# Letting an engine's computed order wait for a far more urgent instruction

## The chip, the cores and the metric

The kernel runs on one core of one Trainium2 chip. The metric is the device time of one execution in microseconds (us); lower is better. The core's engines are PE (TensorE, matrix products), DVE (VectorE), ACT (ScalarE), POOL (GpSimd) and SP (SyncE, which here only issues transfers). Each takes its instructions in the sequence in which the program gives them.

## What is computed

Two trunk layers over 512 latent tokens and 256 context tokens of width 1024. In each layer one projection feeds three attention groups of eight heads and a gate; their results are gated, projected back and added to the stream. Cut to what matters:

```python
def layer(x, cx, ...):
    hx = rmsnorm(x, norm_w) * (1 + scale) + shift        # scale, shift, gate from c @ ada_w + ada_b
    hc = rmsnorm(cx, norm_w) * (1 + scale_c) + shift_c
    px, pc = split_cols(hx @ w_in), split_cols(hc @ w_in)
    ya, yca = global_gqa(...)           # A: all latent and context keys
    yb, ycb = neighbourhood_attn(...)   # B: 2-D window, relative bias
    yc, ycc = window_gqa(...)           # C: +-128 tokens, a sink logit per head
    x = x + gate * ((concat(ya, yb, yc) * silu(px[9])) @ w_out)
    ...                                 # the same for cx, in layer 0 only
    return x, cx
```

After the second layer a final RMSNorm gives the output.

## The kernel before

**The work.** Activations lie transposed (features on partitions, tokens along the free dimension). Every float32 operand of a product is split into a high part, rounded to the matrix format, and a low part, the remainder; a product is three matmuls (high x high, high x low, low x high). So a weight tile of 128x512 is loaded by SP (ws, L254 or L500), rounded by ACT (wh, L245), and its remainder is computed by DVE or POOL (wl, L248). In the output projection of layer 0 some of these tiles are called kept.

An attention unit computes scores on PE into the bank Sbig; DVE scales or masks them and takes the row maximum (P and negm, L1115 to L1117 for group A, L1218 for C, L1278 for B); ACT takes the exponential (L1118, L1221, L1280); SP copies P into a tile of the matrix format (R<-P, L1044); PE transposes R (T, L1049); ACT and DVE make the high and low part (pth L781, ptl L1029); PE multiplies with the values (Obig, L1033). The queries of A and C get their rotary factors on POOL (L951 to L953) with a copy of rotated rows that SP makes (tB<-tA, L950, four issues a tile). At the end of a layer, gated head outputs (u) are loaded again and split (hL, qt, kt and ut, L480 and L481) for the output projection (L508). The modulation vectors of layer 1 are computed on the side, in part as dot products on DVE (junk, L154), over 512 columns in the attention stage and 1024 in the output projection.

The stages in time: a start (to about 97 us) with normalisation and the first projections, the attention of layer 0 woven with the projections of the next heads, its output projection (from about 540 to 660 us), the same for layer 1, and the last output projection and norm.

**What sets the order.** Program text gives only the dependencies. `arrange` (L1950) collects all instructions as `Step` objects with modelled lengths (`busy`, the time for which the engine is taken; `move`, a transfer's length; `ISSUE`, the length of a DMA's issue by its target, 430 ns otherwise). `Graph.run` (L1771) is a simulated execution that places them one by one. For each engine there are two heaps: `later` holds steps whose predecessors are all placed, with the time at which they are ready; `now` holds those that are ready by the engine's current time `t`. The step in `now` with the smallest rank is taken. A step that opens a tile may have to wait for a buffer of its pool (`held`, woken when a buffer comes free). `Graph.back` (L1900) goes through the run backwards and gives each step the time from the end at which it must have started; the negative of it is the next turn's rank, in ns, so a smaller rank means more urgent. The first turn ranks by program priority. This is repeated `turns` = 6 times, and the sequences of the turn that is shortest on paper are fixed as dependencies between neighbours on each engine. PE's sequence comes out of the same run, with a rule of its own that keeps transposes together.

The modelled lengths and delays (`WAIT`, `BEHIND`, `TO_PE`, `TO_LAND`, L1596 to L1600) are constants: the flight of a transfer is a fixed part, its length, and what the other rings take meanwhile.

Of the kernel before, what the change touches and what calls it, by code (L numbers as in the profile page):

```python
# [1594 lines left out]
BANKS = ("pj", "T", "Sbig", "Obig")  # L1595
TO_PE, TO_OTHER, TO_LAND = 400.0, 150.0, 700.0  # L1596
SLOW = 21000.0
ISSUE = dict(tB=580.0, R5=520.0, R2=520.0, wr=680.0)
WAIT = {"PE": 53.0, "POOL": 78.0, "ACT": 36.0, "DVE": 36.0, "SP": 30.0}
BEHIND = {"ACT": 112.0, "DVE": 85.0, "POOL": 45.0}  # L1600
# [13 lines left out]
class Step:  # L1614
# [16 lines left out]
    def cost(self, tiles):  # L1631
# [7 lines left out]
        if self.dma:  # L1639
            b = 4 * outs[0][2][0][1] * size(outs[0][2])  # L1640
            out = stem(outs[0][0].name).split("_")[0]
            far = any(u[0].name not in tiles or tiles[u[0].name][1] for u in ins)
            self.busy = ISSUE.get(out, 430.0)
            self.fixed = 2400.0 if far else 1650.0
# [49 lines left out]
class Graph:  # L1694
# [76 lines left out]
    def run(self, rank):  # L1771

        steps, n = self.steps, len(self.steps)
# [3 lines left out]
        later = {e: [] for e in ENGINES.values()}  # L1777
        now = {e: [] for e in ENGINES.values()}
        free = {e: 0.0 for e in ENGINES.values()}
# [23 lines left out]
        while done < n:  # L1803
            t, e = min((max(free[e], -1.0 if now[e] else later[e][0][0]), e) for e in later if now[e] or later[e])
            free[e] = t = max(t, free[e])
            while later[e] and later[e][0][0] <= t:
                _, r, k = heapq.heappop(later[e])
# [9 lines left out]
                    heapq.heappush(now[e], ((-1e18, 0), min(same)[1]))  # L1817
            r, k = heapq.heappop(now[e])
            s = steps[k]
            need, wait = t, None  # L1820
            for name in self.opens[k]:
                tag = self.tag[name]
# [32 lines left out]
            elif e == "PE":  # L1855
# [5 lines left out]
                if row > 2 and s.switch > 5:  # L1861
                    busy += 20
                if t < SLOW:
                    busy *= 2
# [27 lines left out]
            for j in self.after[k]:  # L1892
                x = fin + self.gap(s, steps[j]) if self.before[j][k] else t
# [175 lines left out]
```

## Time and profile before

| | |
|---|---|
| time, median of 3 runs | 1146.3 us (1142.51 to 1149.14) |
| the profiled execution: time | 1148.5 us |
| the profiled execution: span from first to last instruction | 1146.7 us |
| mean granted clock of TensorE | 0.992 |
| instructions | 21341 |
| bytes moved by DMA | 200.96 MB, mean 175 GB/s |

The profile is one execution. A row of the timeline or of the chain begins with its start and its length in us; then come the engine, the line, the operation, and the tiles written and read (out<-in), and in brackets how long the engine stood idle before it and for whom. A row of the waits names who waited for whom, then the total in us, the number of times and the longest. A row of the windows gives the stretch, its length, and then the busy time of PE, of PE's weight loads (PEld), DVE, ACT and POOL with their instructions, the granted clock, the busy share of the DMA engines and GB/s. Issues of DMAs stand under SPq. Some rows hold several instructions (x3), and their length reaches from the first to the last.

### The profile page before, as it was taken

How to read it: one execution, taken by the hardware profiler on the slowest of the kernel's cores; microseconds unless marked ns; L12 is line 12 of the kernel's file. 1: busy time of each engine (PE TensorE's matmuls, PEld its weight loads, DVE VectorE, ACT ScalarE, POOL GpSimd, SP SyncE). 2: the span in 40 equal slices, each digit the busy share in tenths (PEclk: the TensorE clock that was granted, in tenths of full speed). 3: DMA queues.
4: the chain of work that ended last, by engine and by line, in shares of the span. 5: the costliest groups of instructions: out<-in, count | busy, mean ns of one | idle time of the engine just before them, and what ended most of it. 6: DMA issues, size and time to landing. Idle time of an engine off the chain costs nothing.

```text
span 1146.7 us, 21341 instructions
## 1 busy us (share of the span) xinstructions
PE 1106.9 (97%) x7352; PEld 974.5 (85%) x7352; DVE 778.3 (68%) x1642; ACT 675.8 (59%) x1454; POOL 401.1 (35%) x352
## 2 busy tenths in 40 slices
PE   5999999999999999999899999999999999999996
PEld 3799989998888888888687989998988888888886
DVE  5767667656657777668879764778565567677753
ACT  5546556465656667768623643555556677778651
POOL 1542102145452364526400021221156656556001
PEclk8999999999999999999999999999999999999998
DMA  9455446445464555456768543555344554557452
GB/s 356 180 154 191 140 135 193 137 152 165 157 204 151 191 174 185 160 186 217 252 227 267 166 148 98 169 182 152 126 144 157 161 180 163 194 177 228 140 175 74
DMA packets 111541, 200.96 MB, mean 175 GB/s; under 512 B 13676, under 2 KB 32456, under 8 KB 111432
## 3 DMA queue, kind: packets, MB, share of 16 engines
q1 hardware_dynamic: 103440, 184.01, 49.3%
q10 hardware_dynamic: 7992, 15.58, 4.1%
q8 instruction: 58, 0.95, 0.4%
q14 instruction: 51, 0.42, 0.1%
HBM read 116.46 MB, written 11.25 MB: 111 GB/s over the span
## 4 chain that ended last, share of the span: by engine, by line
PE 79%; DMA 6%; DVE 5%; ACT 3%; issue 3%; POOL 3%; SPq 1%; ACTq 0%; DVEq 0%; POOLq 0%
PE pj L311 29%; PE Obig L1033 9%; PE Sbig L1033 9%; PE T L1049 6%; PE pj L332 6%; PE pj L508 5%; DMA R<-P 4%; PE T L508 4%; PE Sbig L508 2%; PE Sbig L419 2%; PE T L311 2%; PE pj L419 1%; DVE junk L154 1%; PE Sbig L332 1%; DMA dw<-adat_dram 1%
## 5 line engine op out<-in xcount | busy, mean ns | idle before, releaser
L311 PE MATMUL pj<-hL,wh 128*128 128x512 f32 x880 | 293.1, 399 | 0.7 <-ACT tR L995 0.5
L1029 DVE TENSOR_TENSOR ptl<-T,pth 128x512 fp32r<-128x512 f32 (+1 forms) x264 | 172.5, 670 | 70.4 <-ACT pth L781 68.2
L781 ACT ACTIVATE pth<-T 128x512 fp32r<-128x512 f32 (+1 forms) x264 | 147.3, 580 | 73.3 <-PE T L1049 64.4
L311 PEld LDWEIGHTS pj<-hL,wh 128*128 128x128 f32 x880 | 158.8, 188 | 27.3 <-issue 1.7
L311 PE MATMUL pj<-hL,wl 128*128 128x512 f32 x440 | 174.8, 397 | 0.0
L245 ACT ACTIVATE wh<-ws 128x512 fp32r<-128x512 f32 x192 | 119.9, 629 | 93.1 <-PE pj L311 37.4
L1033 PE MATMUL Sbig<-kt,qt 128*128 128x256 f32 (+1 forms) x864 | 159.4, 305 | 0.9 <-DVE negm L1218 0.8
L248 POOL TENSOR_TENSOR wl<-ws,wh 128x512 fp32r<-128x512 f32 x76 | 100.2, 1320 | 145.1 <-ACT wh L245 126.0
L1033 PEld LDWEIGHTS Sbig<-kt,qt 128*128 128x128 f32 x864 | 127.6, 189 | 11.2 <-DVE negm L1218 1.8
L1049 PEld LDWEIGHTS T<-identr,R 128*128 128x128 f32 x1024 | 106.8, 140 | 27.4 <-DMA R<-P 7.4
L1033 PE MATMUL Obig<-pth,vt 128*128 128x256 f32 (+2 forms) x432 | 125.9, 307 | 2.2 <-DVE OT L1069 1.5
L1033 PE MATMUL Obig<-ptl,vt 128*128 128x256 f32 (+2 forms) x432 | 123.8, 306 | 0.2
L1049 PE MATMUL T<-identr,R 128*128 128x128 f32 x1024 | 114.5, 242 | 8.4 <-DMA R<-P 7.2
L248 DVE TENSOR_TENSOR wl<-ws,wh 128x512 fp32r<-128x512 f32 x116 | 84.9, 738 | 40.2 <-ACT wh L245 30.0
L311 PE MATMUL pj<-hC,wh 128*128 128x256 f32 x512 | 98.8, 284 | 0.0
L311 PEld LDWEIGHTS pj<-hL,wl 128*128 128x128 f32 x440 | 82.7, 188 | 15.0 <-issue 0.9
L1033 PEld LDWEIGHTS Obig<-pth,vt 128*128 128x128 f32 x432 | 81.3, 188 | 10.1 <-DVE OT L1069 2.1
L1033 PEld LDWEIGHTS Obig<-ptl,vt 128*128 128x128 f32 x432 | 81.2, 188 | 6.1 <-DVE negm L1117 0.5
L311 PEld LDWEIGHTS pj<-hC,wh 128*128 128x128 f32 x512 | 82.1, 190 | 2.1 <-DVE rs L881 0.2
L1115 DVE CUSTOM_DVE_ANT_0 P<-Sbig,rs 128x768 f32<-128x768 f32 (+1 forms) x80 | 65.7, 845 | 25.5 <-PE Sbig L1033 17.9
L1118 ACT ACTIVATE P<-P,negm 128x768 f32<-128x768 f32 (+1 forms) x80 | 67.5, 846 | 22.5 <-DVE negm L1117 16.7
L1459 POOL TENSOR_TENSOR bm<-wr,bm 128x192 f32<-128x192 f32 (+1 forms) x48 | 41.6, 893 | 97.3 <-DMA bm<-mskB_dram 64.6
(340 smaller groups left out, 2288.4 us busy)
## 6 DMA issues: line engine op xcount, KB each, us to landing
R<-P SPq DMA_DIRECT2D x216, 256.0 KB
ws<-wf_dram SPq DMA_DIRECT2D x120, 256.0 KB
ada<-adaw_dram SPq DMA_DIRECT2D x32, 512.0 KB
ws<-wo_dram SPq DMA_DIRECT2D x57, 256.0 KB
bm<-mskB_dram SPq DMA_DIRECT2D x16, 576.0 KB
R<-P SPq DMA_DIRECT2D x64, 128.0 KB
ws<-wt_dram SPq DMA_DIRECT2D x24, 256.0 KB
tB<-tA SPq DMA_DIRECT2D x72, 64.0 KB
```

The source lines that it names most:

```text
L245: nc.scalar.activation(hi, src, AF.Copy)
L248: eng.tensor_sub(lo, src, hi.bitcast(F32))
L311: nc.tensor.matmul(p[:, 0:n], a[:, r, :], cols(b[kt], c0, n), start=(i == 0), stop=(i == 23))
L332: nc.tensor.matmul(p[:, t * 256:(t + 1) * 256], tok(a[kt], t2 + t), b[:, r, :], start=(i == 0), stop=(i == 23))
L508: nc.tensor.matmul(p[:, 0:n], a[:, r, :], ucols(ua[b][ft], c0, n), start=(ft == FT_ORDER[0] and i == 0), stop=(ft == FT_ORDER[-1] and i == 2))
L781: nc.scalar.activation(out, src, AF.Copy)
L1029: nc.vector.tensor_sub(lo[:, 0:n], T[:, 0:n], hi[:, 0:n].bitcast(F32))
L1033: return nc.tensor.matmul(*args, **kw)
L1049: return nc.tensor.transpose(out.bitcast(F32R), src, identr)
L1115: nc.vector.tensor_tensor_reduce(out=P, in0=S, in1=r.to_broadcast([128, n]), op0=OP.mult, op1=OP.max, scale=1.0, scalar=-3.0e38, accum_out=m)
L1118: nc.scalar.activation(P, P, AF.Exp, bias=nm, accum_out=unit.stat("sums", i))
L1459: nc.gpsimd.tensor_add(b, src, b)
```

## The change

A table `HOLD` gives for DVE, ACT, POOL and SP, but not PE, a gap in rank of 3000 ns. When the run has taken the step with the smallest rank `r` for such an engine, it looks through `later` for steps whose rank is smaller by more than the gap and that become ready before the taken step would end (for a DMA: before the longer of its issue and its transfer would end). If there are any, `x` is the earliest of their times. Among the ready steps (the taken one included), those whose `busy` ends by `x + 60` ns may still go, the most urgent of them first; if there is none, the engine's time is set to `x` and nothing is placed. Everything else is as before: the instructions, the tiles, the number of turns, the choice among them.

```diff
@@ -1595,6 +1595,7 @@
 BANKS = ("pj", "T", "Sbig", "Obig")
 TO_PE, TO_OTHER, TO_LAND = 400.0, 150.0, 700.0
 SLOW = 21000.0
+HOLD = dict(DVE=3000.0, ACT=3000.0, POOL=3000.0, SP=3000.0)
 ISSUE = dict(tB=580.0, R5=520.0, R2=520.0, wr=680.0)
@@ -1817,6 +1818,20 @@
                     heapq.heappush(now[e], ((-1e18, 0), min(same)[1]))
             r, k = heapq.heappop(now[e])
             s = steps[k]
+            if e in HOLD:
+                long = max(s.busy, s.move) if s.dma else s.busy
+                soon = [x for x, y, _ in later[e] if y[0] < r[0] - HOLD[e] and x < t + long]
+                if soon:
+                    x = min(soon)
+                    fit = [z for z in now[e] if t + steps[z[1]].busy <= x + 60]
+                    heapq.heappush(now[e], (r, k))
+                    if not fit:
+                        free[e] = x
+                        continue
+                    r, k = min(fit)
+                    now[e].remove((r, k))
+                    heapq.heapify(now[e])
+                    s = steps[k]
             need, wait = t, None
             for name in self.opens[k]:
                 tag = self.tag[name]
```

## Prediction

> **What bounds the kernel now.** I read the page's busy times first, then who TensorE (PE) waits for, then a table by stage, then the timeline around the stops.
>
> ```profile
> span 1146.7 us, 21341 instructions
> ## 1 busy us (share of the span) xinstructions
> PE 1106.9 (97%) x7352; PEld 974.5 (85%) x7352; DVE 778.3 (68%) x1642; ACT 675.8 (59%) x1454; POOL 401.1 (35%) x352
> ...
> PE Obig L350 <- DVE sq L346: 10.7, 1, 10.7
> PE T L1049 <- DMA R<-P: 7.2, 9, 1.9
> ...
> 97.00:554.00 457.00, 451.87 (x3201) 402.98 (x3199) 319.81 (x708) 294.27 (x657) 178.83 (x151) 1.00 0.53 172
> 554.00:563.00 9.00, 5.73 (x32) 4.34 (x33) 8.89 (x16) 6.53 (x15) 8.26 (x5) 0.98 0.79 282
> 563.00:1088.00 525.00, 515.81 (x3277) 456.99 (x3277) 363.54 (x736) 304.25 (x635) 172.07 (x152) 1.00 0.53 172
> ```
>
> PE is busy for 1106.9 of 1146.7 us, so its idle time is 39.8 us, and no order of the other engines' work can win more than that, apart from clock. The table's columns are length, then busy PE, weight loads, DVE, ACT and POOL, then clock. Between 97 and 1088 us PE stands still for 5.13, 3.27 and 9.19 us, together 17.6. The other 22 us lie at the start (one wait of 10.7 us for the first squares) and in the tail. DVE, ACT and POOL are busy for two thirds of the span or less: an idle moment on them is free unless PE comes to wait for it. So the change acts on 17.6 us of stops, 1.5% of the span, and on whatever new stops it makes.
>
> **What the change does.** A simulated run at build time places the instructions of each engine one by one: of those ready, the one with the longest work behind it. After the change DVE, ACT, POOL and SP look first whether an instruction at least 3 us more urgent becomes ready while the chosen one would run. If so, an instruction that ends by then (60 ns late at most) goes first, or the engine idles until then. No instruction is added or removed and none changes its length; only the sequences differ. On the chip there is no decision to idle: what is left of a hold is that the urgent instruction stands ahead of the lesser one in its queue. A hold therefore gains at most the lesser one's length, and costs when the urgent one arrives later than computed.
>
> **SP.** This is the plainest case, and the largest group of stops (7.2 us in nine).
>
> ```profile
> 931.61 0.90 ACT L1118 ACTIVATE P<-P,negm 128x768 f32<-128x768 f32 x1
> 931.85 1.82 SPq L950 DMA_DIRECT2D tB<-tA  x3
> 932.40 0.20 ACT L1118 ACTIVATION_READ_ACCUMULATOR P<-P,negm 128x1 f32 x1
> 934.16 2.05 SPq L1044 DMA_DIRECT2D R<-P  x3
> 936.14 0.60 ACT L781 ACTIVATE pth<-T 128x512 fp32r<-128x512 f32 x1 [0.90 <-PE T L1049]
> 939.95 0.71 PE L1049 MATMUL T<-identr,R 128*128 128x128 f32 x4 [1.41 <-DMA R<-P]
> 939.97 0.96 DVE L1115 CUSTOM_DVE_ANT_0 P<-Sbig,rs 128x768 f32<-128x768 f32 x1 [2.93 <-DMA R<-P]
> 940.92 0.68 DVE L1029 TENSOR_TENSOR ptl<-T,pth 128x512 fp32r<-128x512 f32 x1
> ```
>
> The exponentials of the first query tile are done at 932.60, but R<-P is issued at 934.16, behind issues of tB (three take 1.82 us, 0.61 each). PE then stops 1.41 us for such an R. A hold puts R<-P ahead of the last of them: R lands up to 0.61 us earlier and tB 0.5 to 0.6 us later. tB feeds the rotary products on POOL, and what covers its delay is the other matmuls woven between; without that cover it would cost 0.6 us itself. Because the fit test counts a DMA's issue (0.43 to 0.58 us in the code) and not its transfer, SP never holds longer than about 0.52 us. For nine stops the bounds are 0 and 9 x 0.61 = 5.5 us. I take five stops and 0.5 us, a gain of **2.5 us**, since some of these R's are late in flight, not in their issue:
>
> ```profile
> 146.97 6.59 DMA R<-P
> 516.40 2.20 DMA R<-P
> ```
>
> The same transfer takes 2.20 us in one place of the chain and 6.59 in another; a hold of half a microsecond does not remove that spread.
>
> **The hand-off of layer 0** (554 to 563 us), with DVE and POOL nearly full:
>
> ```profile
> 555.94 0.58 ACT L781 ACTIVATE pth<-T 128x512 fp32r<-128x512 f32 x1
> 556.24 1.77 DVE L154 CUSTOM_DVE_ANT_0 junk<-dots,sm 128x512 bf16<-128x512 f32 x1
> 557.42 2.28 POOL L481 TENSOR_TENSOR qt<-u,qt 128x768 fp32r<-128x768 f32 x1
> 557.93 0.68 DVE L1029 TENSOR_TENSOR ptl<-T,pth 128x512 fp32r<-128x512 f32 x1
> 559.67 2.94 POOL L481 TENSOR_TENSOR kt<-uf,kt 128x768 fp32r<-128x768 f32 x1
> 562.66 0.80 PE L508 MATMUL pj<-kt,wh 128*128 128x512 f32 x1 [1.42 <-POOL kt L481]
> ...
> 560.00:565.00 5.00, 3.58 (x18) 2.96 (x19) 4.89 (x9) 3.29 (x9) 2.60 (x1) 0.76 0.58 184
> 565.00:570.00 5.00, 5.00 (x21) 4.08 (x20) 3.38 (x11) 0.63 (x1) 0.00 (x0) 0.90 0.60 186
> ```
>
> On DVE a dot product for the next layer's gate (1.77 us here) runs while ptl, which the value matmuls need, has its input from 556.52 on and starts at 557.93: 1.4 us lost to a lesser instruction. On POOL qt runs ahead of kt, but both feed the same output projection, so an urgency gap of 3 us is doubtful there, and the stop of 1.42 us is POOL's. PE loses 3.27 us here, and the granted clock of 0.76 and 0.90 after it costs 0.24 x 5 + 0.10 x 5 = 1.7 us more. Bounds 0 and 5.0; I take a fifth, **1.0 us**, because the longest stop is not an inversion on DVE. The Trainium skill, page "TensorE: Matmul & The Clock Gate", Part 1, lets the clock fall only after an idle window of some 3.4 us. No single stop here comes near that, yet the clock fell. By the page the clock loss would not hang on these stops, the bound would be 3.3, and a fifth of it 0.65 us; the sum would be 0.35 us smaller.
>
> **DVE in the output projection** (598 to 632 us), where it is the fullest engine:
>
> ```profile
> 598.00:632.00 34.00, 32.23 (x155) 26.68 (x154) 32.96 (x55) 10.44 (x18) 0.00 (x0) 1.00 0.83 287
> ...
> 611.67 0.63 ACT L245 ACTIVATE kept<-ws 128x512 fp32r<-128x512 f32 x1
> 612.98 1.28 DVE L154 CUSTOM_DVE_ANT_0 junk<-dw,row,sm 128x1024 bf16<-128x1024 f32 x1
> 614.18 0.69 DVE L248 TENSOR_TENSOR kept<-ws,kept 128x512 fp32r<-128x512 f32 x1
> 614.93 1.20 PE L508 MATMUL Sbig<-hL,kept 128*128 128x512 f32 x4 [1.77 <-DVE kept L248]
> ```
>
> The low half of a weight (kept) has its input at 612.30 and is computed at 614.18, behind a dot product of 1.28 us that is needed much later; PE stops 1.77 us. Bounds 0 and 1.77; I take half a dot, **0.6 us**. The cover is thin: DVE is busy for 32.96 of 34 us, and every idle moment put in moves the dots and the later low halves back.
>
> **ACT, POOL and the rest.** What remains of the 17.6 us is 17.6 - 7.2 - 3.3 - 1.8 = 5.3 us in small stops. Bounds 0 and 5.3; I take a quarter, **1.3 us**. At the start the loads of x are all ready at once, so there is nothing to wait for: 0. In the tail
>
> ```profile
> 1136.61 2.09 POOL L594 TENSOR_TENSOR X<-X,rbl 128x256 f32<-128x256 f32 x3 [3.43 <-ACT rbl L592]
> 1138.15 0.15 DVE L357 TENSOR_SCALAR rstd<-Obig 128x2 f32<-128x2 f32 x1
> 1138.65 0.70 POOL L359 TENSOR_TENSOR rstd<-rstd,mhalf 128x2 f32<-128x2 f32 x1
> ```
>
> rstd stands 0.35 us (1138.30 to 1138.65) behind a product of X. Some 8 us are left there for everything, so a gap of 3 us in urgency is unlikely: I take 0, at most 0.35.
>
> **The new waits.** The same rows show the price. At 937.04 DVE comes to P L1115 and stands for 2.93 us until an R<-P has landed; behind it is ptl L1029, whose input pth was ready at 936.74 and which runs at 940.92. More holds mean more queues in that position: on DVE the value matmuls wait behind it, on ACT the conversions pth and wh, on SP the weight loads. Such a wait reaches PE only where PE has run out of other matmuls. A stop costs PE about 7.2/9 = 0.8 us by the R<-P row, 0.9 with the larger ones counted. I take three new stops, a loss of **2.7 us**; bounds 0 and 20 us (as many new stops as the trace has now, with a little clock). The sequence on PE changes as well, since it is computed in the same run; I take 0 for that and 3 us to either side, from the two long stages, which do like work in different orders and idle 1.1% (5.13 of 457) and 1.75% (9.19 of 525).
>
> **The sum.** 2.5 + 1.0 + 0.6 + 1.3 - 2.7 = 2.7 us gained. The profiled execution took 1148.5 us, 1.8 more than its span; it would take 1145.8. It lies 2.2 above the median of 1146.3, and against that median I forecast **1143.6 us**. Half a per cent, about what a measurement of this kernel can tell from no change, is 5.7 us: 1140.6 to 1152.0 counts as the same.
>
> **Rivals.** (1) *Faster: most stops go.* If a good half of the stops are inversions, as at 612 and 932 us, 9 of 17.6 us go and 1 us of clock: 1146.3 - 10 = 1136. For it: each stop that I followed back has a lesser instruction close ahead. Against it: long flights of R<-P, and POOL's own lengths.
>
> (2) *Slower: queues stand still for what comes late.* The order is computed with fixed flight times, while the chain shows 2.20 and 6.59 us for the same transfer. An engine that waits for the urgent instruction on paper for 0.5 us waits 3 us on the chip, with ready work behind it. Twelve new stops of 0.9 us more than the holds win make 1146.3 + 10.8 = 1157. It decides from about seven such stops net (5.7/0.9). For it: the 2.93 us on DVE above. Against it: most urgent instructions on DVE and ACT wait for PE or each other, not for a DMA. The Trainium skill, "TensorE: Matmul & The Clock Gate", section on the array's architecture, calls the queues of ACT and DVE strictly first in, first out; that speaks for this rival, and the late ptl at 940.92 agrees with it.
>
> (3) *It hardly does what it says.* A hold needs the urgent instruction already known, all its inputs placed in the simulated run, a gap of 3 us, and readiness within 0.4 to 1.3 us; and of six computed orders the one that is shortest on paper is kept. If few holds survive, the time is 1146.3 give or take the 3 us of a reshuffle. Against it: DVE alone has 1642 instructions, and long dots and conversions beside urgent scores are common.
>
> **How the numbers follow.** Forecast 0.36, (1) 0.28, (2) 0.24, (3) 0.12. Forecast and (3) count as the same, 0.48; faster 0.28; slower 0.24. The forecast's own range is 1139 to 1149. For 8 in 10 the range takes in most of both outer cases: 1134 (below 1136, with the reshuffle in part) to 1157, which is (2)'s own price.
>
> **What would show it.** Right: the sum of PE's waits for R<-P falls from 7.2 to about 5 us; R<-P is issued sooner after its exponential than 1.56 us; kept stands ahead of the dot near 613; PE's idle time between 97 and 1088 us is about 15 us; tB and the dots come later. Rival (2) would show as new idle time on DVE, ACT or SP that ends on a DMA, and more PE stops; rival (1) as idle time below 10 us. The prediction is wrong if PE's busy time itself moves by more than 3 us, or if the start or the tail moves by more than 1 us.

## The result, and the profile after

| | before | after |
|---|---|---|
| time, median of 6 runs each | 1145.85 us (1142.51 to 1149.14) | 1135.85 us (1133.38 to 1138.24) |
| ratio to before | 1 | 0.9916, 95% interval 0.9893 to 0.9938 |
| profiled execution: span, clock | 1146.7 us, 0.992 | 1134.2 us, 0.997 |

The change saves 10 us, 0.84% (by the interval 0.62 to 1.07%). In size that is rival (1), not the forecast case. First the head of the page after, then who PE waits for (in all, times, longest):

```profile
span 1134.2 us, 21276 instructions
## 1 busy us (share of the span) xinstructions
PE 1102.6 (97%) x7352; PEld 972.5 (86%) x7352; DVE 769.0 (68%) x1642; ACT 676.3 (60%) x1454; POOL 398.5 (35%) x352
```

```profile
PE Obig L350 <- DVE sq L346: 11.1, 1, 11.1
PE T L1049 <- DMA R<-P: 3.0, 7, 0.8
PE pj L367 <- POOL rstd L359: 1.9, 1, 1.9
PE pj L508 <- POOL hL L481: 1.2, 1, 1.2
PE T L1049 <- DVE ptl L1029: 1.2, 4, 0.4
```

The 65 instructions by which the two heads differ are none of those counted by engine: these numbers are the same in both. PE's idle time (span less busy time) falls from 39.8 to 31.6 us and its busy time by 4.3 us. The waits for R<-P fall from 7.2 to 3.0 us, with the longest 0.8 instead of 1.9; nothing of the same size takes their place.

To see where the time went, the same work must be compared, not the same microseconds. The two tables below are cut at the same five events in each trace: the last matmul of the first projections (L419), the first of layer 0's output projection (L508), the first that uses kept in the bank T, the first projection of layer 1 (L311), and the last transpose of an R (L1049). The columns are the stretch, its length, busy PE, PEld, DVE, ACT, POOL, the clock, the DMA share and GB/s. Before:

```profile
0.00:68.70 68.70, 55.76 (x417) 42.69 (x418) 41.00 (x107) 35.76 (x80) 28.37 (x29) 0.95 0.74 268
68.70:535.70 467.00, 462.52 (x3268) 414.15 (x3266) 323.10 (x712) 294.89 (x656) 179.73 (x155) 1.00 0.52 165
535.70:619.40 83.70, 77.73 (x418) 64.38 (x418) 69.91 (x134) 36.69 (x78) 16.03 (x11) 0.98 0.78 261
619.40:663.00 43.60, 43.60 (x301) 40.59 (x300) 36.90 (x65) 23.77 (x53) 1.02 (x1) 1.00 0.53 168
663.00:1085.70 422.70, 415.55 (x2683) 368.34 (x2681) 281.06 (x585) 264.16 (x552) 171.06 (x151) 1.00 0.51 162
1085.70:1146.70 61.00, 51.70 (x277) 44.35 (x275) 26.38 (x42) 20.50 (x35) 4.86 (x7) 0.94 0.38 124
```

After:

```profile
0.00:69.20 69.20, 56.20 (x417) 42.45 (x418) 41.30 (x107) 35.73 (x81) 27.65 (x28) 1.00 0.74 266
69.20:534.40 465.20, 461.38 (x3267) 413.86 (x3266) 313.37 (x714) 294.05 (x656) 179.73 (x156) 1.00 0.52 167
534.40:611.80 77.40, 75.25 (x418) 63.52 (x417) 69.75 (x129) 36.70 (x79) 15.58 (x11) 1.00 0.83 282
611.80:655.30 43.50, 43.50 (x301) 40.70 (x300) 37.40 (x68) 23.51 (x53) 1.02 (x1) 1.00 0.50 160
655.30:1073.40 418.10, 414.78 (x2683) 367.65 (x2682) 280.65 (x585) 266.06 (x553) 169.67 (x151) 1.00 0.52 164
1073.40:1134.20 60.80, 51.48 (x277) 44.30 (x275) 26.53 (x43) 20.21 (x35) 4.87 (x7) 0.94 0.39 124
```

The start (+0.5 us), the second half of the output projection (-0.1) and the tail (-0.2) are as before. The first attention stage (second row) gives 1.8 us, the hand-off (third row) 6.3, the second attention stage (fifth row) 4.6. In the four middle stretches PE idles 9.3 us instead of 17.6. The hand-off is 84 us long and gives half of what these two executions differ by. That difference is 12.5 us of span and not 10, since the execution shown of the kernel before took 2.6 us more than its median and the one after 0.2. The rows that the prediction quoted there now read, on the engines that matter:

```profile
554.11 0.60 ACT L781 ACTIVATE pth<-T 128x512 fp32r<-128x512 f32 x1
556.14 1.83 POOL L481 TENSOR_TENSOR kt<-uf,kt 128x768 fp32r<-128x768 f32 x1 [1.19 <-ACT kt L480]
556.36 0.67 DVE L1029 TENSOR_TENSOR ptl<-T,pth 128x512 fp32r<-128x512 f32 x1
557.08 0.38 PE L1033 MATMUL Obig<-ptl,vt 128*128 128x256 f32 x1 [0.24 <-DVE ptl L1029]
557.91 2.40 DVE L154 CUSTOM_DVE_ANT_0 junk<-dots,sm 128x512 bf16<-128x512 f32 x1
557.93 1.83 POOL L481 TENSOR_TENSOR qt<-u,qt 128x768 fp32r<-128x768 f32 x1
558.02 0.50 PE L508 MATMUL pj<-kt,wh 128*128 128x512 f32 x1 [0.32 <-POOL kt L481]
```

ptl now stands ahead of the dot product, and kt ahead of qt: PE waits 0.32 us for kt where it waited 1.42. But ptl comes no sooner after its input (554.71) than before: 1.65 us instead of 1.41, now behind other work of DVE, and PE stops 0.24 us for it. On SP, at the place where three issues of tB had stood in front of R<-P:

```profile
926.94 0.18 ACT L1118 ACTIVATION_READ_ACCUMULATOR P<-P,negm 128x1 f32 x1
927.15 3.06 SPq L1044 DMA_DIRECT2D R<-P  x4
928.06 1.12 PE L1049 MATMUL T<-identr,R 128*128 128x128 f32 x7 [0.85 <-DMA R<-P]
```

R<-P is issued 0.03 us after its exponential is done (927.12), not 1.56. The longest stop for an R that is left, 0.85 us (0.8 in the list above), still lies right there.

### The profile page after: what moved, and what is told of

It reads as the page before. It is cut to its first block, busy times and chain, and to the rows that moved or that the text cites. A ratio compares the mean times of both kernels' runs of the same rounds, so it can differ in the third digit from the quotient of the medians.

```text
span 1134.2 us, 21276 instructions
## 1 busy us (share of the span) xinstructions
PE 1102.6 (97%) x7352; PEld 972.5 (86%) x7352; DVE 769.0 (68%) x1642; ACT 676.3 (60%) x1454; POOL 398.5 (35%) x352
## 4 chain that ended last, share of the span: by engine, by line
PE 47%; DMA 4%; ACT 2%; DVE 2%; issue 2%; POOL 2%; SPq 0%; ACTq 0%; DVEq 0%; POOLq 0%
PE pj L311 14%; PE pj L508 5%; PE Obig L1033 5%; PE T L508 5%; PE Sbig L1033 5%; PE Sbig L508 3%; PE T L1049 3%; PE pj L332 3%; DMA R<-P 3%; DMA tB<-tA 1%; PE Sbig L332 1%; PE T L311 1%; ACT P L1118 1%; ACT pth L781 1%; PE T L332 1%
## 5 line engine op out<-in xcount | busy, mean ns | idle before, releaser
L311 PE MATMUL pj<-hL,wh 128*128 128x512 f32 x880 | 291.7, 398 | 0.1
L311 PEld LDWEIGHTS pj<-hL,wh 128*128 128x128 f32 x880 | 158.5, 188 | 25.0 <-issue 0.4
L311 PE MATMUL pj<-hL,wl 128*128 128x512 f32 x440 | 175.0, 398 | 0.0
L1049 PEld LDWEIGHTS T<-identr,R 128*128 128x128 f32 x1024 | 106.3, 140 | 24.3 <-DMA R<-P 5.0
L1049 PE MATMUL T<-identr,R 128*128 128x128 f32 x1024 | 113.3, 242 | 4.9 <-DMA R<-P 3.0
L311 PE MATMUL pj<-hC,wh 128*128 128x256 f32 x512 | 98.8, 284 | 0.0
L311 PEld LDWEIGHTS pj<-hL,wl 128*128 128x128 f32 x440 | 82.7, 188 | 15.3 <-issue 1.3
L1115 DVE CUSTOM_DVE_ANT_0 P<-Sbig,rs 128x768 f32<-128x768 f32 (+1 forms) x80 | 65.7, 845 | 29.3 <-PE Sbig L1033 13.1
L311 PEld LDWEIGHTS pj<-hC,wh 128*128 128x128 f32 x512 | 82.0, 190 | 1.9
L311 PE MATMUL pj<-hC,wl 128*128 128x256 f32 x256 | 72.5, 283 | 0.0
```

The source lines that it names most:

```text
L311: nc.tensor.matmul(p[:, 0:n], a[:, r, :], cols(b[kt], c0, n), start=(i == 0), stop=(i == 23))
L1049: return nc.tensor.transpose(out.bitcast(F32R), src, identr)
L1115: nc.vector.tensor_tensor_reduce(out=P, in0=S, in1=r.to_broadcast([128, n]), op0=OP.mult, op1=OP.max, scale=1.0, scalar=-3.0e38, accum_out=m)
```

## Experiments

The sequence of PE was also different, since the whole order is computed anew. So two theories stood against each other: the holds themselves save the time, or it is the luck of another order, with the holds only as a shake of the dice.

### The hold against the draw

Each experiment splits the six turns, which give the urgencies, from one last simulated run, whose order is used. Holds can be on in the one and off in the other (in e1, e3 and e4 the table is emptied before the turns). The edit is cut to what matters; `hold` is a copy of the table.

```diff
-        if best is None or max(end) < best[0]:
-            best = max(end), streams
+        ranks.append((max(end), rank))
         at = graph.back(start, end, busy)
         rank = [(-t, k) for k, t in enumerate(at)]
+    rank = min(ranks, key=lambda x: x[0])[1]     # e3, e4: ranks[3][1]
+    HOLD.update(hold)                            # e1, e4: on in the last run alone; e2: HOLD.clear()
+    best = None, graph.run(rank)[3]
```

e1: 

> The urgencies are those of the kernel before (its six turns are computed without holds), and only the last simulated run, whose order is used, has holds on all four engines. Theory 1 (holds move urgent instructions ahead of lesser ones, whatever the draw of the order): most of the 10 us between 1145.9 and 1135.9 are gained, so about 1138 us, with the waits of PE for R<-P near 3 us instead of 7.2. Theory 2 (the gain is the luck of another order): the urgencies are the old ones, so 1146 us, within 4 us to either side.

e2: 

> The urgencies are those of the changed kernel (six turns with holds), but the last simulated run, whose order is used, has no holds. Theory 1: most of the gain is lost again, about 1144 us. Theory 2: the luck lies in those urgencies and they are kept, so about 1137 us.

e3: 

> Another draw of the old order: the fourth turn's urgencies instead of the fifth's, no holds at all. It measures how far two orders lie apart without the change. Theory 1: near the kernel before, 1146 us, within 4 us. Theory 2: anything from 1136 to 1152 us; a time below 1140 without a hold would speak strongly for it.

e4: 

> The same fourth turn's urgencies, with holds on in the last simulated run. Theory 1: 5 to 10 us below the same draw without holds, so about 1138 us. Theory 2: no fixed sign against that draw; about as likely above it as below.

The ratios are to the kernel before, measured beside each, with their intervals:

| urgencies from | no hold in the last run | holds in the last run | gain of the hold |
|---|---|---|---|
| before, fifth turn | before itself, 1 (1145.0 us) | e1: 1138.9 us, 0.9946 (0.9929 to 0.9964) | 0.54% |
| before, fourth turn | e3: 1157.1 us, 1.0099 (1.0072 to 1.0126) | e4: 1141.8 us, 0.9985 (0.9969 to 1.0002) | 1.14% |
| the changed kernel | e2: 1149.6 us, 1.0037 (1.0019 to 1.0055) | after: 1135.9 us, 0.9916 (0.9893 to 0.9938) | 1.21% |

With a hold the time is lower in all three rows, by 6 to 14 us (0.0054 to 0.0121 of 1145), and no interval of a row overlaps its neighbour's. Theory 2 fails as it was put: the old urgencies with holds gain, the new ones without holds are slower than before. But the draw counts as well: without holds the three orders lie 11 us apart, and the order of the kernel before is the best of them. The 10 us of the change are thus a hold worth 13.9 us on urgencies that are 4.2 us worse without it.

Two reservations belong to this. Three pairs of one sign come by chance one time in eight; the engines' runs below add to the evidence. And two of the orders without holds are not such as the kernel without holds would take: the fourth turn is not the one that is shortest on paper, and the urgencies of e2 come from turns with holds. Against the order that it does take, the holds gave 6.2 us on the same urgencies (e1) and 10 us on their own, so 14 us is the upper end.

The stretches of the tables above, cut at the same events in the three pairs, show where (one execution of each, in us):

| without and with holds | first attention stage | hand-off | second attention stage | PE idle in the four middle stretches |
|---|---|---|---|---|
| before, e1 | 467.0, 467.7 | 83.7, 77.9 | 422.7, 416.0 | 17.6, 12.7 |
| e3, e4 | 469.1, 465.4 | 88.8, 80.8 | 422.0, 418.3 | 22.9, 12.3 |
| e2, after | 469.5, 465.2 | 80.4, 77.4 | 420.5, 418.1 | 15.7, 9.3 |

The hand-off, the second attention stage and PE's idle time become shorter in all three pairs, the first attention stage in two. On the changed kernel's own urgencies the hand-off gives 3.0 us, less than the first attention stage (4.3); the rest of its 6.3 us above came with the other urgencies.

Several expectations of theory 1 missed: e3 was to lie within 4 us of before, e2 at 1144, and e4 5 to 10 us below e3, not 13. The time depends on the draw far more than I had allowed; e3 is even beyond the 1152 us of theory 2. In e1 PE's waits for R<-P were to be near 3 us; they are 5.0.

### Which engine

e5 to e8 keep the urgencies of the changed kernel and delete all but one engine from the table for the last run. Their measure is e2, the same without any hold.

```diff
     rank = min(ranks, key=lambda x: x[0])[1]
+    for e in [e for e in HOLD if e not in ("DVE",)]:     # e6 ACT, e7 POOL, e8 SP
+        del HOLD[e]
     best = None, graph.run(rank)[3]
```

e5: 

> The urgencies of the changed kernel; in the last simulated run only DVE holds. Without any hold these urgencies gave 1149.6 us, with all four 1135.9. Theory 1a (the gain is mostly DVE's, where long dots and low halves stand ahead of ptl and P): about 1140 us. Theory 1b (the gain is mostly SP's, where R<-P stands behind other issues, as the prediction's largest term had it): about 1148 us.

e6: 

> The same urgencies, only ACT holds. Theory 1a: a small part, about 1147 us. Theory 1b: about 1147 us. A third theory (1c: the exponentials and pth on ACT wait behind the rounding of weights and the gates) gives about 1141 us.

e7: 

> The same urgencies, only POOL holds. Few instructions on POOL feed PE soon, so all theories give about 1149 us, within 3 us; a gain of over 5 us would mean that the length of POOL's instructions (1.3 to 2.9 us each) counts for more than their number.

e8: 

> The same urgencies, only SP holds. Theory 1a: a small part, about 1147 us. Theory 1b: most of the gain, about 1140 us, with PE's waits for R<-P falling from 4.4 us to under 2.

| hold on | time | ratio to before | less than e2's 1.0037 by |
|---|---|---|---|
| DVE (e5) | 1139.6 us | 0.9953 (0.9932 to 0.9974) | 0.84%, 9.6 us |
| ACT (e6) | 1148.5 us | 1.0030 (1.0012 to 1.0047) | 0.07%, 0.8 us |
| POOL (e7) | 1146.4 us | 1.0010 (0.9991 to 1.0029) | 0.27%, 3.1 us |
| SP (e8) | 1145.4 us | 1.0003 (0.9984 to 1.0022) | 0.34%, 3.9 us |

Each difference is uncertain by some 0.25 to 0.28% (the half-widths of the two intervals, added in squares), about 3 us. DVE's hold is the one that matters: theory 1a. SP's and POOL's are small and just above that uncertainty, ACT's can't be told from nothing. The four gains sum to 17.4 us, more than the 13.9 of all holds together, so they are not independent shares, and each is one order measured against one other order. What speaks for DVE beyond that: all eight orders of this document in which DVE holds take 1135.9 to 1144.9 us, and all six in which it does not take 1145.0 to 1157.1, though e4 and e11, the longest of the eight, can't be told from the kernel before. In e8 PE's waits for R<-P did not fall below 2 us. In e2 and then in e8 they read:

```profile
PE T L1049 <- DMA R<-P: 4.4, 8, 1.2
```

```profile
PE T L1049 <- DMA R<-P: 5.0, 7, 1.4
```

What DVE's hold removes can be seen in e2 at the hand-off, where the old fault is back. The rows are in order of time:

```profile
556.94 0.74 DVE L154 CUSTOM_DVE_ANT_0 junk<-dots,sm 128x512 bf16<-128x512 f32 x1
557.61 1.02 DVE L1374 SCALAR_TENSOR_TENSOR OT<-OT,u 128x256 f32<-128x256 f32 x2
558.55 1.01 DVE L1029 TENSOR_TENSOR ptl<-T,pth 128x384 fp32r<-128x384 f32 x2
559.15 0.54 PE L1049 MATMUL T<-identr,R 128*128 128x128 f32 x4 [0.67 <-DVE ptl L1029]
```

A dot product and two scalings of finished outputs run first, and PE stops for ptl, which frees the bank that the next transposes need. With DVE's hold alone (e5) the dot is gone from there, the scalings still stand first, and PE stops 0.21 us:

```profile
550.37 1.02 DVE L1374 SCALAR_TENSOR_TENSOR OT<-OT,u 128x256 f32<-128x256 f32 x2
551.31 1.01 DVE L1029 TENSOR_TENSOR ptl<-T,pth 128x384 fp32r<-128x384 f32 x2
551.91 0.54 PE L1049 MATMUL T<-identr,R 128*128 128x128 f32 x4 [0.21 <-DVE ptl L1029]
```

The same stretch of work, first in e2, then with DVE's hold alone (e5):

```profile
540.00:620.40 80.40, 76.05 (x417) 64.60 (x416) 70.36 (x135) 36.26 (x78) 14.70 (x11) 0.98 0.81 271
```

```profile
534.50:611.40 76.90, 75.05 (x418) 63.21 (x417) 70.19 (x129) 35.83 (x76) 15.60 (x11) 1.00 0.82 282
```

PE idles 4.35 us in the one and 1.85 in the other, with DVE as full as before (70.2 us). The prediction had feared that idle moments on a full DVE would push the dots and the low halves back; no stop of PE for a kept weight shows in e5.

### Which lesser instructions on DVE

Both runs keep the edit of e5, in which only DVE holds, and let the hold apply to some of the lesser instructions alone.

```diff
+            spare = s.kind == "InstMemset" or any(w and stem(x.name).startswith("junk") for x, w, _, _, _ in s.use)
-            if e in HOLD:
+            if e in HOLD and spare:      # e9; e10: and not spare
```

e9: 

> The urgencies of the changed kernel; only DVE holds, and only where the lesser instruction is a dot product into junk or a memset that opens a bank. Without holds 1149.6 us, with all of DVE's holds 1139.6. If the dots ahead of ptl and of the weights' low halves cost the time, as the prediction read it at 556 and 613 us: 1142 us or less, with the stretch from the first output projection matmul to the first that uses kept in the bank T falling from 80.4 to below 78 us. If it is the low halves and copies: about 1148 us.

e10: 

> The complement: only DVE holds, and only where the lesser instruction is neither a dot product nor a memset (low halves wl, copies of kt, scalings). If those stand in the way, in the attention stages above all: about 1141 us, with the 469.5 us of the first attention stage and the 420.5 us of the second falling by some 3 us each. If it is the dots: about 1148 us.

e9 takes 1143.1 us, ratio 0.9976 (0.9957 to 0.9995); e10 1142.5 us, 0.9975 (0.9960 to 0.9989). Against e2 each gives 0.61 or 0.62%, 7 us, and DVE's whole hold gave 9.6: both kinds stand in the way. That their gains overlap is likely but barely shown, since the two together exceed the whole by 4 us, uncertain by 4. Neither expectation came true as a whole. In e9's profile the stretch from the first output projection matmul to the first use of kept in T is 80.0 us, not below 78; its span of 1143.9 us is close to e2's 1145.3, so this execution shows little of the gain and not its place. In e10 the first attention stage is 463.6 us, 5.9 shorter than e2's 469.5, but the second one 422.2, 1.7 longer. Which instructions carry how much stays open.

### The gap, and a version without ACT

```diff
-HOLD = dict(DVE=3000.0, ACT=3000.0, POOL=3000.0, SP=3000.0)
+HOLD = dict(DVE=1000.0, ACT=1000.0, POOL=1000.0, SP=1000.0)     # e11
+HOLD = dict(DVE=3000.0, POOL=3000.0, SP=3000.0)                 # e12
```

e11: 

> The change with a gap of 1 us instead of 3 us in all six turns. If smaller inversions matter too: 1 to 4 us below the changed kernel's 1135.9, about 1133 us. If waiting for barely more urgent instructions wastes the engines or meets late arrivals: above 1139 us.

e12: 

> The change without ACT's hold, in all six turns. By the single engines ACT's hold gave 1.1 us of the 13.7, so this should be equal to the changed kernel within 2.5 us, 1133 to 1138 us. If ACT's hold matters beside DVE's (its conversions feed what DVE waits for): 1140 us or more.

e11 takes 1144.9 us, 0.9985 (0.9964 to 1.0006): a smaller gap gives the gain away. In the execution shown, the longest of its ten (1148.5 us), PE's waits for R<-P are longer than in any other kernel here:

```profile
PE T L1049 <- DMA R<-P: 8.7, 11, 2.2
```

That is what waiting for instructions that are hardly more urgent would do, but it is one draw, and draws with holds lie 6 us apart (1135.9 to 1141.8); e11 is 3 us outside them. So the loss is measured, its cause only argued. e12 takes 1137.4 us, 0.9930 (0.9907 to 0.9952): equal to the change within the intervals, as expected. No version here beat the changed kernel.

## Why the prediction was right or wrong

The measured 1135.9 us lies in the range of 1134 to 1157, and the sign was right. But the likeliest case was put at 1143.6 us with a gain of 2.7, and the half per cent was passed: it was rival (1), whose 1136 us is what came. That its figure fits to a microsecond is luck. It counted half of the stops of the old order; what came is a hold worth up to 13.9 us on a new order that is 4.2 us worse without it.

**The bound held.** 17.6 us of stops were there to be won in the middle, 8.3 of them went. Start and tail moved by 0.5 us or less, as said.

**The hand-off was mis-sized.** Two terms lay there, 1.0 us for the stops between 554 and 563 us and 0.6 for kept, 1.6 together; the stretch that holds both became 6.3 us shorter, 3.8 of it idle time of PE. The prediction had the fault (a dot product ahead of ptl, another ahead of kept) and took a fifth and a third of the bounds. The two stops that it named went nearly whole: kept's 1.77 us is gone, kt's 1.42 fell to 0.32. (The dot was not the whole delay of kept: between its input at 612.30 and the dot DVE also computed xn, L561, 0.75 us.) On the old draws the holds remove kept's stop (1.8 us in before, none in e1; 1.4 and 0.4 in e3, none in e4); on the new urgencies it is gone without holds too (e2). kt is no mark of the holds: without them it stands ahead of qt in e2 and e3, and with them behind it in e4. The doubt whether the gap applies there was thus not refuted.

The clock loss, 1.7 us, was counted in the bound, and a fifth of it taken; in the execution after it is gone (0.98 to 1.00 over the hand-off). That is one execution of each, and those of the kernel before alone have mean clocks between 0.990 and 0.998, so it isn't shown that the order did it. Nor is the hold's gain made of clock: e1 gained 6.2 us with a median clock of 0.994, the same as before's beside it. Whether a misplaced instruction on a full engine costs more than the stop it shows, by delaying all behind it, remains open.

**SP was the wrong engine to rank first.** Its term was 2.5 us with a bound of 5.5. The waits for R<-P fell by 4.2 us from before to after, but 2.8 of that came with the other urgencies alone (7.2 in before, 4.4 in e2). In the three pairs the holds took 2.2 (7.2 to 5.0), 1.5 (4.1 to 2.6) and 1.4 us (4.4 to 3.0), so the size was not far off. The engine was: with SP's hold alone the waits were 5.0 us against e2's 4.4, and its time gained 3.9 us, uncertain by 3. DVE's hold alone (e5) brought these waits to 2.6 us. That fits row maxima that come late on DVE, so that R<-P can only be issued late; no run here shows it directly.

```profile
PE T L1049 <- DMA R<-P: 2.6, 3, 1.0
```

**The loss of 2.7 us did not come the way it was argued.** Three new stops of 0.9 us were to come from queues that wait for late arrivals. In the middle of the span some of PE's waits did grow: for hL from POOL by 0.8 us, for ptl by 0.9, for the row maximum m of L1115 by 0.4, for pth by 0.1, together 2.2. None of these is a wait for a DMA, and whether the holds made them isn't shown. The idle time that ended on a DMA, the sign named for rival (2), did not grow: between 60 and 1090 us it went from 16.4 to 12.4 us on DVE and from 28.7 to 27.4 on ACT. So rival (2) failed. Rival (3) did too.

**The reshuffle was put far too small.** I took 3 us from the idle shares of two stages of one order. e3 is another order from the same program without any hold and lies 11.3 us away (0.0099 of 1145). Shares inside one order say nothing on how far another order can fall. PE's busy time moved by 4.3 us, which had been named as a sign that a step was wrong: 2.5 of it lie in the hand-off (77.73 to 75.25), and of these 1.7 are the cost reckoned for the lower clock of the execution before. Nor did every instruction keep its length: DVE's same 1642 instructions took 9.3 us less in all (778.3 to 769.0), without any hold in e2 766.7; why isn't shown.

## What to carry to other kernels

In a kernel whose main engine is 97% busy, look for a less urgent instruction that starts just before an urgent one is ready, first on the engine that is fullest in the worst stage. Letting DVE, ACT, POOL and SP wait for the urgent one paid 6 to 14 us of 1145 here, three times out of three, where the gap in urgency was 3 us; DVE alone paid 9.6 the one time it was tried. When an order is computed anew by a change, measure the rule on several draws (rule on and off with the same urgencies), since two draws without it differed by as much as the rule was worth. Compare two orders stage by stage at the same events, and ask of each stop that is gone whether it is also gone in an order without the rule: kt's was.

## What the runs showed of the hardware

TensorE's granted clock fell where PE had only short stops. In the kernel before it was 1.00 up to 562.60 us and 0.50 for the 3.40 us behind it, after stops of 0.84, 0.41, 0.70 and 1.42 us within nine us, the last of which ends at 562.66:

```profile
553.80:562.60 8.80, 5.41 (x32) 3.99 (x31) 8.69 (x17) 6.13 (x14) 8.45 (x5) 1.00 0.83 296
562.60:566.00 3.40, 3.34 (x8) 2.67 (x9) 3.40 (x9) 1.35 (x4) 0.00 (x1) 0.50 0.74 230
```

In e8 it was this, with no stop longer than 1.48 us in the ten us around:

```profile
550.00:555.00 5.00, 4.58 (x20) 3.67 (x21) 4.47 (x10) 4.61 (x12) 2.34 (x2) 0.70 0.94 273
```

The total of the stops does not decide it either: the clock over the hand-off was 1.00 with 2.15 us of stops (after) and 0.98 with 4.35 (e2), but 1.00 with 4.27 (e10). Each of these is one execution; what does decide it is not shown.
